# Encoder layer on one core: token tiles 4 to 7 normed column-major in PSUM, fourth block sum in PSUM banks, decay rates and token passes laid elsewhere

## The chip, the core and the metric

One core of a Trainium2 chip. The kernel is written against five engines that run side by side, each with its own queue in program order: TensorE (PE in the profile, its weight loads PEld), VectorE (DVE), ScalarE (ACT), GpSimd (POOL) and SyncE (SP, which here only issues DMAs). The metric is the device time of one execution in microseconds, median of several runs.

## The reference, cut to what matters

1024 tokens (a grid of 16 rows by 64 columns) of 1024 channels, float32. First an embedding LayerNorm, then one layer:

```
h    = layer_norm(x, emb_ln_g, emb_ln_b)
proj = h @ w_in                # 1024 x 5120: q | k | v | z_attn | u | z_lru | g_attn | g_lru
y_a  = neighbourhood_attention(q, k, v, rpb) * silu(z_attn)       # 8 heads x 64
u    = centred_depthwise_conv(u)
a    = exp(-8 * softplus(-lam) * sigmoid(gate_r(u)))              # decay of the recurrence
y_b  = (rg_lru forward + rg_lru backward)(u) * silu(z_lru)
m    = sigmoid(g_attn + b0) * (y_a @ w_ba) + sigmoid(g_lru + b1) * (y_b @ w_bb)
out  = layer_norm(alpha * h + m @ w_out, ln_g, ln_b)
```

Two things are wanted of h: column-major (channels on the partitions) as the operand of the projection, and row-major in DRAM, for `alpha * h` at the very end. The factor `8 * softplus(-lam)` (the decay rates) depends on the weights alone.

## The kernel before

**Tiles and stages.** The tokens form eight tiles of 128. Each float32 operand of a product is kept as a high part (rounded to fp32r) and a low part (the rest); a product is three matmuls, high x high, low x high, high x low (`mm3`, L127 is the subtraction that makes a low part, L133 the matmul). The projection of 34 of the column groups runs as 17 *pairs*; a pair is one 2 x 2 block product done with seven block products in place of eight. These need sums of blocks of h (T1 to T4, made once) and of the weights (s1 to s4, made for each pair).

**First stage, to about 83 us.** Tile by tile: statistics on DVE (`ln_stats`, `ln_rstd`), then the normalization. Tiles 0, 1 and 3 do it on DVE (`ln_v`); tiles 2 and 4 to 7 scale on ACT (`ln_scale`, L254) and take gain and shift on POOL (`ln_g`, four 512-wide operations, L260). `keep` stores the row-major tile to `h_d`. `turn` has TensorE transpose the tile in eight 128 x 128 steps into two PSUM banks (tile name tp, L271), ACT writes the high parts (`turn_hi`) and DVE the low parts (`turn_lo`) to the block operands B11, B12, B21, B22. For tiles 4 to 7 `t_full` makes T1, T2 and T3 and `t_last` makes T4, on DVE; `t_hi` splits on ACT and `t_lo` on POOL. In between stand the products for v (`v_part`, L327) and for half of q (`q_part`), which need nothing but finished tiles, and the splitting of the first pair's weights (`s_hi`, `s_lo`).

**The pairs, from about 83 us.** A loop over *slots*: slot 7p + k is block product k of pair p, in the order a11, a12, s2, s1, s3, s4, a22. In each slot the code issues, in this order: the copy or sum that empties the PSUM bank of the slot before (`evacuate`), the high part of a weight block of the next pair (`s_hi`), what `at(slot, 0, ...)` has put there, the product, the low part of the block of the slot before (`s_lo`), the stores that fell due two slots after their sum, a weight sum of the next pair (`s_sum`, L385) or, at k = 4, the weight loads of the pair after it, and what `at(slot, 1, ...)` has put there. Six PSUM banks serve the pairs, and two the gates of the recurrence. Product a22 adds into the bank of which `evacuate` has just read in the slot before.

**Order.** All queues are written out by hand: `manual_schedule` for PE and for DVE, ACT, POOL and SP; an instruction waits for its data at the head of its queue, with all behind it. The lists `CONV_AT`, `GATE_AT`, `LATE_AT` and `range(8, 14)` for the decay rates say in which slots the side work is issued: the convolution (`conv_stage`, from slot 14), the gates and the scans (`gate_stage`, from slot 21), the decay rates (`decay_rates`, L650 to L670, 31 operations on 8 or 16 columns on DVE and one Exp on ACT, in six portions). The first `take` (`take_q`) splits q of the other heads: sum on DVE, high part on ACT one slot later, low part on DVE and store two slots later.

**After the pairs** come attention, the merge and the output projection, which the change doesn't touch; there `z_load` reads `h_d` back.

Of the kernel before, what the change touches and what calls it, by code (L numbers as in the profile page):

```python
# [15 lines left out]
P = 128  # L16
# [27 lines left out]

BIAS_W = 7 * P

SM_CW, SM_CB, SM_GB, SM_LAM, SM_BM, SM_N = 0, 16, 20, 36, 44, 60
# [17 lines left out]


@with_exitstack
def encoder_kernel(ctx, tc, x, gb1, gb, w_qk, w_v, w_s, w_ba, w_bb, w_gate, smalls, bias, w_out, out):
    nc = tc.nc
    V, A, G, PE, SP = nc.vector, nc.scalar, nc.gpsimd, nc.tensor, nc.sync  # L70

# [39 lines left out]
    V.memset(eps_t, EPS)  # L111
    V.memset(eps_z, EPS * TWICE * TWICE)
    A.activation(warm, eps_t, AF.Sqrt)
    sm = cst.tile([P, SM_N], F32, name="sm")
# [11 lines left out]
    def lo_of(eng, lo, full, hi):  # L126
        eng.tensor_tensor(lo, full, hi.bitcast(F32), ALU.subtract)  # L127
# [48 lines left out]
    def qk_prep(m):  # L176
        qk_hi(m)
        qk_lo(m)
# [52 lines left out]
    def ln_sums(i):  # L231
        ln_stats(i)
        ln_root(i)
# [15 lines left out]
    def ln_scale(i):  # L249

        z, (st, mv, sd, ve) = xs[i], sts[i]
        ln_rstd(i)
        V.tensor_scalar(ve[:, 2:3], mv[:, 0:1], -1.0, sd, ALU.mult, ALU.mult)
        A.activation(z[:], z[:], AF.Identity, bias=ve[:, 2:3], scale=sd)  # L254

    def ln_g(i):
        z = xs[i]
        for c in range(2):
            for w, op in enumerate((ALU.mult, ALU.add)):
                G.tensor_tensor(z[:, halves[c]], z[:, halves[c]], gb_t[w][c][:], op)  # L260

    def keep(i):
        SP.dma_start(h_d[i], xs[i][:])

    tps = {}

    def turn(i, kk):
# [22 lines left out]
    def f(t, i):  # L290
        return t[:, :, ti(i)].bitcast(F32)

    def t_full(i):

        tag = ("a22", "a21", "a12", "a22")[i - 4]
        tt[i, 3] = wsp.tile([P, 4, P], F32, tag=tag, bufs=2 if tag == "a22" else 1, name=f"t3_{i}")[:]
# [3 lines left out]
        A.copy(t3, tp4(i, 0))  # L300
        V.tensor_tensor(t1, tp4(i, 0), f(B11[0], i), ALU.subtract)
        V.tensor_tensor(t1, t1, f(B11[1], i), ALU.subtract)
        V.tensor_tensor(t2, tp4(i, 1), t1, ALU.subtract)
        V.tensor_tensor(t3, tp4(i, 1), t3, ALU.subtract)

    def t_last(i):
        t4 = tt[i, 4] = tt[i, 2]
        V.tensor_tensor(t4, f(B21[0], i), t4, ALU.subtract)
        V.tensor_tensor(t4, t4, f(B21[1], i), ALU.add)

    def t_hi(i, *cs):
        for c in cs:
            A.copy(Ts[c][0][:, :, ti(i)], tt[i, c])  # L313

    def t_lo(i, *cs):
        for c in cs:
            lo_of(G, Ts[c][1][:, :, ti(i)], tt[i, c], Ts[c][0][:, :, ti(i)])

    vos, vn = {}, {}

    def v_part(i, kind, ks):

        if i not in vos:
            vos[i], vn[i] = bank(f"v{i}"), 0
        for k in ks:
            a = blocks[k // 4][i // 4][kind == "a"][:, k % 4, ti(i)]
            PE.matmul(vos[i][:], a, wv[kind == "w"][k][:], start=vn[i] == 0, stop=vn[i] == 23)  # L327
            vn[i] += 1
# [39 lines left out]
    def s_load(p, *names):  # L368
        for z, o in enumerate(names if p < N_PAIR else ()):
            if p:  # L370
                t = wsp.tile([P, 4, P], F32, tag=o, bufs=2 if o == "a22" else 1, name=f"{o}_{p}f")[:]
            else:
                if z == 0:
                    place = dict(pool=ln, tag="x", bufs=5) if o == "a21" else dict(pool=wpl, tag="ws", bufs=1)
                    both = place.pop("pool").tile([P, 2, 4, P], F32, name=f"{o}_{p}f", **place)
# [11 lines left out]
    def s_hi(p, o):  # L387
        if p < N_PAIR:
            s_w[p, o] = pair(wsp, [P, 4, P], f"w{o}_{p}", tag="w" + o)
            (G.tensor_copy if p and o in HI_POOL else A.copy)(s_w[p, o][0][:], s_a[p, o])  # L390

    def s_lo(p, o):
        if p < N_PAIR:
            hi, lo = s_w[p, o]
            lo_of(G if p and o in LO_POOL else V, lo[:], s_a[p, o], hi[:])


    K0, K1, KS, BOTH = range(4), range(4, 8), range(8), range(2)
# [10 lines left out]
    load_x(3)  # L409
    load_x(4)  # L410
    SP.dma_start(sm[:], smalls)

    warm_up(WARM[0])
    PE.transpose(clock[:, 256:272], gb_row[:], ident[:16, :16])
# [82 lines left out]
    for c, pl in zip((4, 3, 1, 2), hts):  # L497
        Ts[c] = pair(pl, [P, 4, HALF], f"ht{c}", tag=f"ht{c}")
    T1, T2, T3, T4 = (Ts[c] for c in (1, 2, 3, 4))

    def turned_in(i, kk):
        banks[0] = pst
        turn(i, kk)
        turn_hi(i, kk)
        banks[0] = ps0

    def tile_in(i):
        for kk in BOTH:
            turned_in(i, kk)

    def tile_lo(i):
        for kk in BOTH:
            turn_lo(i, kk)

    def ln_next(i):
        ln_sums(i)
        ln_scale(i)
        ln_g(i)

    keep(2)  # L520
    keep(3)
    turned_in(2, 0)
# [3 lines left out]
    v_store(0)  # L526
    turned_in(2, 1)
    turned_in(3, 1)
    ln_scale(4)
    ln_g(4)  # L530
    qk_prep(1)
    tile_lo(2)
    tile_lo(3)
    v_lo(1)
    v_store(1)
    load_x(7)
    ln_next(5)
    for kind in "hwa":
        v_part(2, kind, KS)
    keep(4)  # L540
    ln_next(6)
    v_hi(2)
    for kind in "hw":
        v_part(3, kind, KS)
    v_lo(2)
    v_store(2)
    keep(5)
    tile_in(4)
    tile_lo(4)
    ln_next(7)  # L550
    v_part(3, "a", KS)
    t_full(4)
    v_hi(3)
    v_lo(3)
    v_store(3)
    keep(6)
    q_part(0, 0, slice(256, HALF))
    tile_in(5)
    q_hi(0, 0)
    t_hi(4, 2, 1, 3)  # L560
    t_lo(4, 2, 1, 3)
    tile_lo(5)
    q_lo(0, 0)
    q_store(0, 0)
    keep(7)
    t_full(5)
    q_part(1, 0)
    q_hi(1, 0)
    q_lo(1, 0)
    q_store(1, 0)  # L570
    t_hi(5, 2, 1, 3)
    t_lo(5, 2, 1, 3)
    for kind in "hwa":
        v_part(4, kind, KS)
    tile_in(6)
    v_hi(4)
    tile_lo(6)
    v_lo(4)
    v_store(4)
    t_full(6)  # L580
    t_hi(6, 2, 1, 3)
    t_lo(6, 2, 1, 3)
    for kind in "hwa":
        v_part(5, kind, KS)
    s_load(0, "a11", "a12")
    tile_in(7)
    v_hi(5)
    tile_lo(7)
    v_lo(5)
    v_store(5)  # L590
    t_full(7)
    t_hi(7, 2, 1, 3)
    t_lo(7, 2, 1, 3)
    s_load(0, "a21", "a22")
    s_load(1, "a21")
    for kind in "hwa":
        v_part(6, kind, KS)
    v_hi(6)
    v_lo(6)
    v_store(6)  # L600
    s_load(1, "a12")
    s_sum(0, "s1", "s2", "s3", "s4")
    for kind in "hwa":
        v_part(7, kind, KS)
    v_hi(7)
    v_lo(7)
    v_store(7)
    s_load(1, "a11")
    for o in OPS[:3]:
        s_hi(0, o)  # L610
        s_lo(0, o)
    q_part(0, 1)
    for o in OPS[3:5]:
        s_hi(0, o)
        s_lo(0, o)
    q_hi(0, 1)
    q_lo(0, 1)
    q_store(0, 1)
    s_load(1, "a22")
    q_part(1, 1)  # L620
    for o in OPS[5:]:
        s_hi(0, o)
        s_lo(0, o)
    t_last(4)
    q_hi(1, 1)
    t_hi(4, 4)
    t_last(5)
    q_lo(1, 1)
    q_store(1, 1)
    for i in (5, 6, 7):  # L630
        if i > 5:
            t_last(i)
        t_hi(i, 4)
    for i in (7, 4, 5, 6):
        t_lo(i, 4)
# [5 lines left out]

    ev = pool("ev", "right")
    lru = pool("lru", "right")
    sp = lru.tile([P, 8], F32, name="sp")
    nsp = lru.tile([P, 8], F32, name="nsp")
    t0, t1, t2 = (lru.tile([P, 8], F32, name=f"sp{c}") for c in range(3))
    lam = sm[:, SM_LAM:SM_LAM + 8]

    def decay_rates():
# [144 lines left out]
    def gate_stage(t, d, slot):  # L794
# [36 lines left out]
            A.activation(g["w"][:], g["w"][:], AF.Sqrt)  # L831

        def tables():
            A.activation(warm[:], eps_t[:], AF.Sigmoid)

        def inputs():
            first = S - 1 if d else 0
# [109 lines left out]
    def gates_b(j):  # L947
# [2 lines left out]
    takes = [take_q, lambda: take_u(0), lambda: take_zg(zb_d, 0, "zb"), lambda: take_zg(za_d, 0, "za"), gates_a(0), gates_a(1),  # L950
             lambda: take_u(2), gates_b(0), lambda: take_zg(zb_d, 2, "zb"), gates_a(2), gates_b(1),
             lambda: take_k(0), gates_a(3), lambda: take_k(2), lambda: take_zg(za_d, 2, "za"), gates_b(2), gates_b(3)]
    rates = decay_rates()
# [809 lines left out]
```

## Time and profile before

| | us |
|---|---|
| median of 3 runs | 662.94 (662.82 to 663.04) |
| the profiled execution | 663.5 |
| its span in the trace | 661.7 |
| TensorE busy in it | 649.5 |
| DVE, ACT, POOL busy in it | 521.6, 389.0, 396.7 |

The span runs from the first to the last instruction that the profiler saw; 1.8 us of the execution's time lie around it. A row of a timeline has start, duration, engine, line, operation, output <- inputs, shapes and count, and in brackets the idle time of the engine before it with what ended it. A row of a group has the count, then busy time in us and mean ns of one, then idle time before. A row of the chain has start, duration and what ran.

### The profile page before, as it was taken

Reading aid. Unit: us, or ns where it says so; the run is one execution under the profiler, and the core shown is the slowest. Engines: PE = TensorE matmul, PEld = TensorE weight load, DVE = VectorE, ACT = ScalarE, POOL = GpSimd, SP = SyncE. Lnnn points to the kernel's source line nnn. Section 1 sums busy time; section 2 is a strip of 40 time slices with the busy share of each in tenths; the row PEclk is TensorE's granted clock in tenths of the full one; section 3 lists DMA queues with packets and bytes.
Section 4 is the critical chain, followed back from the end, with each engine's and each line's share of the span. In section 5 each row is a group of like instructions: output and inputs, shape, how many; then the busy total and the mean of one; then the engine's idle time right before and its main releaser. Section 6 shows DMA issues by size and latency. Waiting matters only on the chain.

```text
span 661.7 us, 9464 instructions
## 1 busy us (share of the span) xinstructions
PE 649.5 (98%) x3119; PEld 543.5 (82%) x3119; DVE 521.6 (79%) x860; ACT 389.0 (59%) x686; POOL 396.7 (60%) x311
## 2 busy tenths in 40 slices
PE   8999999999999999999999999999999999999994
PEld 7888888888888887888788888888898888888883
DVE  7978867786899599879987696277877876994776
ACT  5564433356786677777666834277777744573242
POOL 6799263434676476658556455013552549989857
PEclk9999999999999999999999999999999999999998
DMA  8747607033334133532361548898977298333023
GB/s 324 271 140 250 195 33 257 15 111 128 125 113 135 57 112 99 188 111 81 132 220 59 192 163 281 306 342 272 362 264 240 68 306 294 113 113 127 24 104 128
DMA packets 52482, 113.42 MB, mean 171 GB/s; under 512 B 5505, under 2 KB 9937, under 8 KB 50897
## 3 DMA queue, kind: packets, MB, share of 16 engines
q1 hardware_dynamic: 51968, 112.28, 49.0%
q8 instruction: 25, 0.41, 0.2%
q10 hardware_dynamic: 464, 0.53, 0.2%
q14 instruction: 25, 0.20, 0.1%
HBM read 77.11 MB, written 35.68 MB: 170 GB/s over the span
## 4 chain that ended last, share of the span: by engine, by line
PE 86%; DVE 7%; POOL 2%; issue 1%; ACT 1%; DMA 1%; POOLq 0%; DVEq 0%; ACTq 0%
PE a L133 32%; PE s L133 12%; PE mb L133 12%; PE x L133 6%; PE w L133 5%; PE v L327 4%; PE s L1107 3%; PE acc L1155 3%; PE pt L1129 3%; PE q L133 2%; PE g L805 2%; POOL x L260 1%; DVE ws_l L127 1%; DVE uc L763 1%; PE tp L271 1%
## 5 line engine op out<-in xcount | busy, mean ns | idle before, releaser
L133 PE MATMUL a<-ht_h,ws_h 128*128 128x512 f32 x136 | 53.1, 391 | 0.0
L133 PE MATMUL a<-ht_l,ws_h 128*128 128x512 f32 x136 | 52.9, 389 | 0.0
L133 PE MATMUL a<-ht_h,ws_l 128*128 128x512 f32 x136 | 52.9, 389 | 0.0
L133 PE MATMUL a<-b_l,wa_h 128*128 128x512 f32 x136 | 52.9, 389 | 0.0
L133 PE MATMUL a<-b_h,wa_h 128*128 128x512 f32 x136 | 52.9, 389 | 0.0
L133 PE MATMUL a<-b_h,wa_l 128*128 128x512 f32 x136 | 52.9, 389 | 0.0
L1117 DVE CUSTOM_DVE_ANT_0 sc<-s,bias 128x384 f32<-128x384 f32 (+1 forms) x64 | 33.5, 523 | 20.3 <-PE s L1107 11.4
L1136 ACT CAST pt_h<-pt 128x384 fp32r<-128x384 f32 x64 | 29.0, 453 | 23.8 <-PE pt L1129 19.3
L1122 ACT ACTIVATE p<-sc,summ 128x384 f32<-128x384 f32 (+1 forms) x64 | 37.9, 592 | 5.4 <-DVE summ L1117 5.0
L133 PE MATMUL mb<-ya,wb_h 128*128 128x512 f32 x128 | 39.7, 390 | 0.1
L913 POOL CAST wb_h<-wb 128x512 fp32r<-128x512 f32 x9 | 7.0, 781 | 47.2 <-DMA wb<-in_w_bb_dram 47.2
L127 DVE TENSOR_TENSOR pt_l<-pt,pt_h 128x384 fp32r<-128x384 f32 x64 | 33.3, 520 | 1.9 <-ACT pt_h L1136 1.6
L127 POOL TENSOR_TENSOR ht_l<-t,ht_h 128x512 fp32r<-128x512 f32 x16 | 21.9, 1406 | 18.2 <-ACT ht_h L313 18.2
L1521 POOL TENSOR_TENSOR z<-z,gb 128x512 f32<-128x512 f32 (+2 forms) x23 | 27.7, 1218 | 8.5 <-ACT z L1516 7.5
L327 PE MATMUL v<-wv,b_h 128*128 128x512 f32 x128 | 32.4, 395 | 0.4 <-ACT b_h L426 0.4
L1107 PE MATMUL s<-ks,qs 128*128 128x384 f32 (+1 forms) x128 | 31.7, 329 | 0.0
L133 PEld LDWEIGHTS a<-ht_h,ws_h 128*128 128x128 f32 x136 | 25.5, 188 | 5.9 <-issue 0.5
L1129 PEld LDWEIGHTS pt<-ident,p 128*128 128x128 f32 x176 | 23.1, 140 | 8.3
L133 PEld LDWEIGHTS a<-ht_l,ws_h 128*128 128x128 f32 x136 | 25.5, 188 | 5.3
L133 PEld LDWEIGHTS a<-b_h,wa_l 128*128 128x128 f32 x136 | 25.5, 188 | 5.3
L133 PEld LDWEIGHTS a<-b_h,wa_h 128*128 128x128 f32 x136 | 25.5, 188 | 5.3
L133 PEld LDWEIGHTS a<-b_l,wa_h 128*128 128x128 f32 x136 | 25.5, 188 | 5.3
(542 smaller groups left out, 2258.9 us busy)
## 6 DMA issues: line engine op xcount, KB each, us to landing
ks<-k_d SPq DMA_DIRECT2D x8, 1024.0 KB, 7.6
h_d<-x SPq DMA_DIRECT2D x8, 512.0 KB, 2.9
v_d<-vs SPq DMA_DIRECT2D x8, 512.0 KB, 3.2
q_d<-q SPq DMA_DIRECT2D x8, 512.0 KB, 3.2
ga_d<-ga SPq DMA_DIRECT2D x16, 256.0 KB, 2.1
gb_d<-gb SPq DMA_DIRECT2D x16, 256.0 KB, 2.4
k_d<-k SPq DMA_DIRECT2D x8, 512.0 KB, 5.1
qs<-q_d SPq DMA_DIRECT2D x8, 512.0 KB, 5.2
```

The lines of the kernel that those rows point to most:

```text
L127: eng.tensor_tensor(lo, full, hi.bitcast(F32), ALU.subtract)
L133: PE.matmul(o, a, b, start=first and i == 0, stop=last and i == len(prods) - 1, skip_group_check=not (first and last))
L327: PE.matmul(vos[i][:], a, wv[kind == "w"][k][:], start=vn[i] == 0, stop=vn[i] == 23)
L805: PE.matmul(o[:, n, :], w[:, 2 * d + b, :], us[b][:, n * HALF:(n + 1) * HALF], start=z == 0, stop=z == 1)
L913: G.tensor_copy(hi[:], st[:])
L1107: PE.matmul(o[:, :P * len(near(t))], q[:, t * P:(t + 1) * P], k[:, z, keys], start=z == 0, stop=z == 1)
L1117: V.tensor_tensor_reduce(s[:, :w], o[:, :w], heads[h][2][:, b0:b0 + w], -1.0, 3.0e38, ALU.add, ALU.min, accum_out=sums[h][0][:, t:t + 1])
L1122: A.activation(probs[h % 2][t][:], scs.pop((h, t))[:, :w], AF.Exp, bias=sums[h][0][:, t:t + 1], scale=-1.0, accum_out=sums[h][1][:, t:t + 1])
L1129: PE.transpose(tp[:, n * P:(n + 1) * P], probs[h % 2][t][:, z * P:(z + 1) * P], ident[:])
L1136: A.copy(pt[0][:, span(b)], tps[h, b][:, :P * len(near(b))])
L1155: PE.matmul(acc[n][:, lo - n * HALF:hi - n * HALF], vvs[h // 2][:, b, h % 2, :], pt[:, a:a + hi - lo], start=b in (1, 6) and z == 0, stop= ...
L1521: G.tensor_tensor(z, z, gbs[c, n][:, part], (ALU.mult, ALU.add)[c])
```

## The change

1. **Tiles 4 to 7 column-major.** x of these tiles is also given to the kernel transposed (`xt`; `load_xt`). The statistics still come from row-major tiles. `spread` has TensorE turn the column of means and that of reciprocal deviations into two 128 x 128 blocks of one PSUM bank (two transposes); `spread_copy` copies the second to SBUF; `centred` subtracts the mean on DVE (from PSUM) and multiplies on POOL; `affine` applies gain and shift on ACT, now a scale and a bias for each partition, eight 128-column activations into PSUM. From there `turn_hi` and `turn_lo` go on as before. 32 transposes of tiles go, as do `ln_scale` and `ln_g` for these tiles.
2. **Row-major h of tiles 4 to 7, later.** In the slots of `TOKENS_AT` x is loaded once more (`tokens_in`), scaled on ACT with the kept statistics (`tokens_scaled`), given gain and shift on POOL in four 512-wide operations, one a slot, slots 4 to 19 in all (`tokens_gained`), and stored (`tokens_out`). The gain and shift rows are loaded in slot 1 (`gains_in`).
3. **The fourth block sum** (T4) is formed in four PSUM banks and not in SBUF; its low parts move from POOL to DVE, the high part of tile 7 from ACT to DVE. The highs of T1 to T3 of tiles 4 and 5 move from ACT to POOL.
4. **Decay rates** in slots 4 to 9 and not 8 to 13; their tiles lie in the constants' pool.
5. **Weights of the first pairs:** lows of a22 and s4 of pair 0 on POOL, highs of a12 and s2 of pair 1 on ACT.
6. The order of the first stage is written anew around this: all of v for tiles 4 to 7 stands behind q of the first half.

```diff
+TOKENS_AT = ((1, 3, (4, 5, 6, 7)), (2, 6, (8, 9, 10, 11)), (9, 11, (12, 13, 14, 15)), (9, 12, (16, 17, 18, 19)))
+RATES_AT = (4, 5, 6, 7, 8, 9)
+FIRST_POOL = ("a22", "s4")
+FIRST_ACT = ((1, "a12"), (1, "s2"))
...
+    def spread(i):
+        bcp[i] = pst.tile([P, HALF], F32, tag="bank", name=f"bcp{i}")
+        for z, col in enumerate((sts[i][1][:, 0:1], sts[i][2])):
+            PE.transpose(bcp[i][:, z * P:(z + 1) * P], col.to_broadcast([P, P]), ident[:])
+    def spread_copy(i):
+        bcs[i] = wsp.tile([P, 1, P], F32, tag=f"s{i - 3}", name=f"bc{i}")
+        A.copy(bcs[i][:, 0], bcp[i][:, P:2 * P])
+    def centred(i):
+        for kk in range(2):
+            t = xts[i][:, 4 * kk:4 * kk + 4, :]
+            V.tensor_tensor(t, t, bcp[i][:, :P].unsqueeze(1).to_broadcast([P, 4, P]), ALU.subtract)
+            G.tensor_tensor(t, t, bcs[i][:].to_broadcast([P, 4, P]), ALU.mult)
+    def affine(i, *kks):
+        for kk in kks or BOTH:
+            tps[i, kk] = pst.tile([P, HALF], F32, tag="bank", name=f"tp{i}_{kk}")
+            for k4 in range(4):
+                k = 4 * kk + k4
+                g, b = (sm[:, SM_LN + 8 * z + k:SM_LN + 8 * z + k + 1] for z in range(2))
+                A.activation(tps[i, kk][:, k4 * P:(k4 + 1) * P], xts[i][:, k, :], AF.Identity, bias=b, scale=g)
+            turn_hi(i, kk)
...
-    def t_last(i):
-        t4 = tt[i, 4] = tt[i, 2]
-        V.tensor_tensor(t4, f(B21[0], i), t4, ALU.subtract)
-        V.tensor_tensor(t4, t4, f(B21[1], i), ALU.add)
+    def t_last(i, *steps):
+        for step in steps or BOTH:
+            V.tensor_tensor(tt[i, 4], (f(B21[0], i), tt[i, 4])[step], (tt[i, 2], f(B21[1], i))[step],
+                            (ALU.subtract, ALU.add)[step])
     def t_hi(i, *cs):
         for c in cs:
-            A.copy(Ts[c][0][:, :, ti(i)], tt[i, c])
+            (V.tensor_copy if (i, c) == (7, 4) else G.tensor_copy if i < 6 and c < 4 else A.copy)(Ts[c][0][:, :, ti(i)], tt[i, c])
     def t_lo(i, *cs):
         for c in cs:
-            lo_of(G, Ts[c][1][:, :, ti(i)], tt[i, c], Ts[c][0][:, :, ti(i)])
+            lo_of(G if c < 4 else V, Ts[c][1][:, :, ti(i)], tt[i, c], Ts[c][0][:, :, ti(i)])
...
+    for i in (7, 6, 5, 4):
+        tt[i, 4] = pst.tile([P, HALF], F32, name=f"t4_{i}")[:].rearrange("p (k t) -> p k t", k=4)
...
+    def tokens_scaled(i):
+        n = 2 * i - 8
+        A.activation(hw[i][:], hw[i][:], AF.Identity, bias=kept[:, n:n + 1], scale=kept[:, n + 1:n + 2])
+    def tokens_gained(i, z, c):
+        t = hw[i][:, halves[c]]
+        G.tensor_tensor(t, t, ln_row[z][:, halves[c]], (ALU.mult, ALU.add)[z])
...
+    for i, tag, (s0, s1, later) in zip(range(4, NT), ("a", "uc", "uc", "a"), TOKENS_AT):
+        at(s0, 1, lambda i=i, tag=tag: tokens_in(i, tag))
+        at(s1, 1, lambda i=i: tokens_scaled(i))
+        for slot, (c, z) in zip(later, itertools.product(BOTH, BOTH)):
+            at(slot, 1, lambda i=i, z=z, c=c: tokens_gained(i, z, c))
+        at(later[-1] + 1, 1, lambda i=i: tokens_out(i))
     rates = decay_rates()
-    for slot in range(8, 14):
+    for slot in RATES_AT:
         at(slot, 1, lambda: next(rates))
```

More of the change, by code (lines that the diff above doesn't have):

```diff
@@ L113, in encoder_kernel @@
     A.activation(warm, eps_t, AF.Sqrt)
+    kept = cst.tile([P, 8], F32, name="kept")
+    sp, nsp, t0, t1, t2 = (cst.tile([P, 8], F32, name=f"sp{c}") for c in range(5))
     sm = cst.tile([P, SM_N], F32, name="sm")
@@ L372, in s_load @@
             else:
-                if z == 0:
-                    place = dict(pool=ln, tag="x", bufs=5) if o == "a21" else dict(pool=wpl, tag="ws", bufs=1)
-                    both = place.pop("pool").tile([P, 2, 4, P], F32, name=f"{o}_{p}f", **place)
+                if z == 0 and o == "a11":
+                    both = wpl.tile([P, 2, 4, P], F32, tag="ws", bufs=1, name="a11_0f")[:]
+                elif z == 0:
+                    both = both_xt[0][:, 1].rearrange("p (z k) f -> p z k f", z=2)
                 t = both[:, z]
@@ L536, in encoder_kernel @@
     load_x(7)
[L537 to L541, printed above, removed]
-    v_hi(2)
-    for kind in "hw":
-        v_part(3, kind, KS)
+    load_xt(6)
+    load_xt(7)
+    v_part(2, "h", KS)
+    v_part(2, "w", KS)
+    spread(4)
+    spread_copy(4)
+    centred(4)
+    qk_prep(1)
+    stats_t(5)
+    v_part(2, "a", KS)
+    v_part(3, "h", KS)
+    v_part(3, "w", K0)
+    spread(5)
+    spread_copy(5)
+    stats_t(6)
+    centred(5)
+    v_hi(2)
+    v_part(3, "w", K1)
+    v_part(3, "a", K0)
+    spread(6)
+    spread_copy(6)
+    affine(4, 0)
+    ln_sums(7)
+    centred(6)
     v_lo(2)
     v_store(2)
[L547 to L552, printed above, removed]
+    affine(4, 1)
+    sts_rest(7)
+    v_part(3, "a", K1)
     v_hi(3)
+    lows_t(4)
     v_lo(3)
     v_store(3)
-    keep(6)
     q_part(0, 0, slice(256, HALF))
-    tile_in(5)
-    q_hi(0, 0)
+    t_full(4)
+    t_places(1, 2, 3)
     t_hi(4, 2, 1, 3)
     t_lo(4, 2, 1, 3)
-    tile_lo(5)
+    affine(5)
+    q_part(1, 0)
+    spread(7)
+    q_hi(0, 0)
     q_lo(0, 0)
     q_store(0, 0)
-    keep(7)
+    spread_copy(7)
+    centred(7)
+    lows_t(5)
     t_full(5)
-    q_part(1, 0)
+    t_hi(5, 2, 1, 3)
+    t_lo(5, 2, 1, 3)
+    affine(6)
     q_hi(1, 0)
@@ L570, in encoder_kernel @@
     q_store(1, 0)
[L571 to L575, printed above, removed]
+    affine(7)
+    lows_t(6)
+    t_full(6)
+    s_load(0, "a11", "a12")
+    for i in (4, 5):
+        for kind in "hwa":
+            v_part(i, kind, KS)
     v_hi(4)
-    tile_lo(6)
+    v_hi(5)
+    t_hi(6, 2, 1, 3)
+    t_lo(6, 2, 1, 3)
+    s_load(0, "a21", "a22")
     v_lo(4)
     v_store(4)
[L580 to L588, printed above, removed]
+    s_load(1, "a21")
     v_lo(5)
     v_store(5)
+    lows_t(7)
     t_full(7)
[L592 to L595, printed above, removed]
     for kind in "hwa":
@@ L600, in encoder_kernel @@
     v_store(6)
+    t_hi(7, 2, 1, 3)
+    t_lo(7, 2, 1, 3)
     s_load(1, "a12")
@@ L612, in encoder_kernel @@
     q_part(0, 1)
-    for o in OPS[3:5]:
+    for o in ("s1", "s3", "a22", "s4"):
         s_hi(0, o)
         s_lo(0, o)
+    t_places(4)
+    T1, T2, T3, T4 = (Ts[c] for c in (1, 2, 3, 4))
+    pst.release()
+    pst = tc.alloc_tile_pool(name="pst4", bufs=1, space=bass.MemoryType.PSUM, reuse_waits="tile")
+    for i in (7, 6, 5, 4):
+        tt[i, 4] = pst.tile([P, HALF], F32, name=f"t4_{i}")[:].rearrange("p (k t) -> p k t", k=4)
     q_hi(0, 1)
@@ L1733 @@
         "x": np.stack([xg[rows, cols].reshape(P, D) for rows, cols in TILES]),
+        "xt": np.stack([xg[rows, cols].reshape(P, NK, P).transpose(2, 1, 0) for rows, cols in TILES[4:]]),
         "gb1": np.stack([g["emb_ln_g"], g["emb_ln_b"]])[None],
```

104 lines of the change are left out of this document (64 added, 40 removed).

## The prediction

> **What bounds the kernel now.** I read the page first (busy shares, chain), then TensorE's waits, then the stretches.
>
> ```profile
> span 661.7 us, 9464 instructions
> ...
> PE 649.5 (98%) x3119; PEld 543.5 (82%) x3119; DVE 521.6 (79%) x860; ACT 389.0 (59%) x686; POOL 396.7 (60%) x311
> ...
> PE 86%; DVE 7%; POOL 2%; issue 1%; ACT 1%; DMA 1%; POOLq 0%; DVEq 0%; ACTq 0%
> ```
>
> ```profile
> PE tp L271 <- POOL x L260: 0.4, 1, 0.4
> PE a L133 <- DVE w L838: 0.4, 1, 0.4
> ```
>
> TensorE works 649.5 of 661.7 us and, after the first 10 us, waits twice for 0.4 us. So a TensorE instruction taken out is worth its own time, and any wait put in costs its full length. The other engines have room, though it isn't the same everywhere:
>
> ```profile
> 40.00:60.00 20.00, 19.63 (x102) 16.53 (x101) 16.54 (x29) 10.62 (x20) 19.61 (x15) 1.00 0.59 212
> 60.00:80.00 20.00, 20.00 (x94) 16.66 (x93) 15.28 (x22) 10.39 (x20) 9.47 (x8) 1.00 0.52 170
> 80.00:100.00 20.00, 20.00 (x88) 16.16 (x88) 14.55 (x21) 6.13 (x11) 11.42 (x10) 1.00 0.20 70
> 100.00:120.00 20.00, 20.00 (x90) 16.52 (x89) 15.64 (x48) 5.39 (x9) 5.91 (x8) 1.00 0.64 221
> ```
>
> Columns: stretch, length, busy time of PE, PEld, DVE, ACT, POOL, clock, DMA share, GB/s. POOL is full at 40 to 60 us (the gain and shift of tiles 4 to 7) and nearly free at 100 to 120, where the change puts that work.
>
> **The change, part by part.** *TensorE, removed.* 32 transposes (eight for each of tiles 4 to 7); added: 8 that spread a tile's mean and rstd.
>
> ```profile
> 4.21 3.41 PE gps L212 x16
> ...
> 53.95 0.87 PE tp L271 x8
> 54.82 5.47 PE v L327 x24
> 60.30 0.88 PE tp L271 x8
> ...
> 91.15 2.72 PE s L133 x12
> ...
> 99.31 11.18 PE a L133 x48
> ```
>
> In the chain eight transposes take 0.88 us, so 0.11 each: 4 x 0.88 = 3.5 us go. The added ones are of the kind of gps (a column broadcast), 0.21 each there, at a time when everything on TensorE ran at half its later rate; between 8 x 0.11 = 0.9 and 8 x 0.21 = 1.7 I take 0.9, since they stand amid full-rate work. Net -2.6.
>
> *TensorE's waits ahead of the pairs.* This one goes with POOL's passes (-0.37):
>
> ```profile
> 42.38 0.66 PE L271 MATMUL tp<-ident,x 128*128 128x128 f32 x4 [0.37 <-POOL x L260]
> ```
>
> A new one takes its place. spread(6) needs tile 6's statistics, and they stand on DVE behind those of tile 5:
>
> ```profile
> 24.90 1.28 DVE L223 BATCH_NORM_STATS2 ln4t<-x 128x6 f32<-128x512 f32 x2
> 28.01 2.47 DVE L127 TENSOR_TENSOR b_l<-tp,b_h 128x512 fp32r<-128x512 f32 x4
> 31.00 1.27 DVE L223 BATCH_NORM_STATS2 ln5t<-x 128x6 f32<-128x512 f32 x2
> 33.38 0.21 DVE L239 TENSOR_SCALAR ln5e<-ln5e 128x1 f32<-128x1 f32 x1
> ```
>
> A 512-wide DVE step is 2.47/4 = 0.6, a tile's statistics to rstd 33.59 - 31.00 = 2.6. DVE from 24.9: statistics 4 1.6, v 0.6, small ones 1.0, four lows 2.4, v 0.6, centring tile 4 1.2, tile 5 2.6, copies 0.2, tile 6 2.6: 37.7. TensorE from 25.0: 16 transposes 1.7, 44 of the products at 5.47/24 = 0.23 10.0, two spreads 0.45: 37.2. So about +0.45 (0 to 1). Behind that wait stand v of tile 3 and all that follows; the last spread waits for DVE's reading of tile 4's bank (t_full), which by the same count ends just ahead. Net of both: +0.1.
>
> *ACT* loses four 1024-wide scalings and six high copies (to POOL), and gains 32 of 128 columns.
>
> ```profile
> 26.59 0.30 ACT L229 ACTIVATE ln4e<-ln4m,few 128x1 f32<-128x1 f32 x1
> 28.13 1.24 ACT L254 ACTIVATE x<-x,ln4e 128x1024 f32<-128x1024 f32 x1 [0.27 <-DVE ln4e L253]
> ...
> L280 ACT CAST b_h<-tp 128x512 fp32r<-128x512 f32 x15 | 8.2, 590 | 5.4 <-PE tp L271 5.4
> ```
>
> No row has 128 columns: between 0.30 (one column) and 0.59 (512); on the line between the two rows of scalings, 0.30 + 127/1023 x 0.94 = 0.42, which I take. 13.4 us added, 8 removed, over 50 us in which ACT is half idle: nothing, and if that cover were gone, up to 5 us. ACT begins tile 4 behind the third spread, near 38; a tile is 8 x 0.42 and three copies at 0.5, so 4.9, and six other copies stand between: tile 7 ends near 38 + 19.6 + 3 = 61. v of tile 7 is due at 37.7 and 0.23 of spread, 4 + 24 products of tile 3 and q at 0.23 with 24 of 256 columns at half that (9.3), another spread and three tiles at 5.5: 63.8. So it is in time by 2 to 3 us.
>
> *DVE* gains eight centrings, four lows of the fourth sum (from POOL) and a high copy, 13 x 0.6 = 7.8, and gives two weight lows to POOL (1.2): +6.6 over the 60 us in which it waited some 13. The fourth sums stand behind the last q, and their PSUM banks are asked for only in slot 3 of the pairs, 8 us on: 0 (up to +1).
>
> *The pairs.* From here a slot is one product of 2.72 us. Four `a` products from 99.31 took 11.18 where 4 x 2.72 is 10.88: a22 of pair 0 waits for a late DVE, itself late by POOL's lows of the fourth sum. With these gone, -0.25 (0 to -0.3). Now the moved work: POOL has a 512-wide token operation in each of slots 4 to 19, and the decay rates' 31 small DVE operations come in slots 4 to 9. Each is hidden if one looks at busy shares only. The rows around speak against it (columns: start, duration, engine, line):
>
> ```profile
> 94.14 1.29 POOL L127 TENSOR_TENSOR wa_l<-a_1f,wa_h 128x512 fp32r<-128x512 f32 x1
> 95.37 3.12 POOL L390 CAST ws_h<-s_1f 128x512 fp32r<-128x512 f32 x3
> ...
> 110.61 0.61 POOL L390 CAST ws_h<-s_2f 128x512 fp32r<-128x512 f32 x1 [0.85 <-POOL wa_l L127]
> 113.34 0.62 POOL L390 CAST ws_h<-s_2f 128x512 fp32r<-128x512 f32 x1 [2.11 <-PE s L133]
> ```
>
> ```profile
> 94.21 1.76 DVE L127 TENSOR_TENSOR wa_l<-a_1f,wa_h 128x512 fp32r<-128x512 f32 x1 [4.22 <-POOL wa_h L390]
> 95.90 1.10 DVE L385 TENSOR_TENSOR s_1f<-a_1f,s_1f 128x512 f32<-128x512 f32 x1
> 96.92 1.09 DVE L127 TENSOR_TENSOR ws_l<-s_1f,ws_h 128x512 fp32r<-128x512 f32 x1
> ...
> 110.66 0.58 DVE L657 TENSOR_TENSOR sp<-sp,sp 128x8 f32<-128x8 f32 x1
> 113.17 0.17 DVE L662 TENSOR_TENSOR sp<-sp,sp 128x8 f32<-128x8 f32 x1
> 113.37 0.61 DVE L663 TENSOR_SCALAR sp<-sp 128x8 f32<-128x8 f32 x1
> ```
>
> A DVE operation on SBUF alone that comes while POOL works ends just behind POOL's: 94.21 + 1.76 = 95.97 behind 95.43, and two 8-column operations of 0.17 become 0.58 and 0.61, ending at 111.24 and 113.98 behind 111.22 and 113.96. POOL's casts in turn take 1.04 for 0.62. The two take turns. [...]
>
> [...] The two rows of small ones are nearest, and both were blocked to the end: I take 5.5. Two places pass it on to TensorE: s1 of pair 1 (slot 10) takes a PSUM bank of pair 0, and a22 of pair 1 (slot 13) needs DVE's sum of slot 12; queued behind them on TensorE is all the rest.
>
> Slots 14 to 20 hold the first convolution as well, three taps of 1.3 us on SBUF alone, with POOL's last six token operations: +0.8 (0 to 2.7), since DVE had these 3 us of waiting there:
>
> ```profile
> 123.69 1.28 DVE L763 SCALAR_TENSOR_TENSOR uc<-up,sm,uc 128x1024 f32<-128x1024 f32 x1 [1.03 <-ACT uc L759]
> 126.91 0.70 DVE L696 TENSOR_TENSOR a<-u,a 128x512 f32<-128x512 f32 x1 [1.94 <-PE a L133]
> ```
>
> A TensorE that stood still for over 5 us may start again at half rate, as gps did: 0 to 3.4 (half of the 7 us from its start to the end of gps); I take 1. [...]
>
> *SP's queue.* Six more loads and no fewer stores: x of tile 4 column-major ahead of the first h store, which had waited for the DMA queue anyway; in slot 9 the load of tile 7's rows waits until tile 4's store has landed (one buffer), and behind it stand the weights of pair 3 in slot 11.
>
> ```profile
> h_d<-x SPq DMA_DIRECT2D x8, 512.0 KB, 2.9
> ```
>
> 2.9 us is little more than a slot, and weights are asked for five slots ahead: 0; without that lead, 3 us once.
>
> *Sum.* -2.6 + 0.1 - 0.25 + 5.5 + 0.8 + 1.0 = +4.6. The profiled execution took 663.5 (661.7 span and 1.8 around it), 0.6 above the median of the runs; against the median, 662.9 + 4.6 = **667.5 us**.
>
> **The rivals.**
>
> [...] DVE's small operations slip between POOL's, or DVE runs far enough ahead: for it, both engines' busy shares at 80 to 120 us (78% and 30 to 57%); against it, the two blocked rows. -2.6 + 0.1 - 0.25 = -2.75: 660.2 us.
>
> *They cancel* (no change). POOL's operations hold DVE only in part and TensorE waits 2 to 4 us in all, with no half rate: about 662.9. [...]
>
> *The column-major tiles come late* (slower). It is ACT's 128-column operations at 0.6, the price of 512 columns: 32 x 0.6 = 19 us, 5.8 more than counted, and tile 7 ends near 67 where v of tile 7 is due at 63.5. It decides from 0.5 us each; at 0.6 some 3.3 us of waiting less 2.75: 663.5. With the statistics late as well (the upper 1 us), 664.3, which is slower by 0.2%.
>
> *The saving isn't one*: TensorE ahead only waits longer for DVE at the 0.4 us of L838. For it, that chain runs over DVE; against it, it begins behind a TensorE product, so it moves along. 662.5.
>
> **How the numbers follow.** A measurement of this kernel tells about 0.2%, 1.3 us, from no change. Forecast 0.55 (own range 664 to 672), port without effect 0.28, cancelled 0.10, late tiles 0.04, no saving 0.03. Faster: 0.28 and a part of the cancelled, 0.30. Slower: 0.55, nearly all of it, and half of the late tiles, 0.57. Same: 0.13. Two signs hold most, so the range goes from the bottom of the fast case to the forecast's upper bounds less the least likely tenth: 659.6 to 671.5.
>
> **What would show it.** Right: TensorE 2 to 3 us earlier at the first `a` product on split weights (80 us instead of 82.8); one wait of 0.3 to 0.8 at the spreads; then one wait of several us for DVE between 105 and 125 us, with small DVE operations of 0.5 to 1.3 us from 94 on, each ending behind a POOL operation, and matmul steps above 0.23 after it. Wrong: DVE's small operations at 0.17 to 0.2 beside busy POOL rows, and no TensorE wait there; then the time is near 660. A wait for ACT in front of v of tiles 4 to 7 would mean the late tiles.

## The result and the profile after

The changed kernel took 672.53 us (median of 6 runs, 670.96 to 674.87) where the kernel before took 662.89 on the same chip: a ratio of 1.0149, with a 95% interval of 1.0129 to 1.0169. It is 9.6 us slower (8.6 to 11.2); the forecast was 4.6 slower, and its range ended at 671.5. Runs of the changed kernel spread over 4 us, those of the kernel before over 0.3. The profiled execution, at 673.9, is 1.4 above its median; its span is 10.4 us longer than before's, and that is what the rows have to account for.

The page of the changed kernel (span; busy time, share and instructions; granted clock in tenths over 40 slices; shares of the chain that ended last):

```profile
span 672.1 us, 9492 instructions
...
PE 651.9 (97%) x3095; PEld 543.2 (81%) x3095; DVE 546.7 (81%) x875; ACT 401.6 (60%) x717; POOL 412.2 (61%) x321
...
PEclk9999999789999999999999999999999999999998
...
PE 67%; DVE 20%; issue 5%; ACT 3%; DMA 2%; POOL 1%; SPq 0%; POOLq 0%; DVEq 0%; ACTq 0%
```

VectorE is now 20% of the chain that ended last (7% before), and the clock row has a dip to 7 and 8 in the eighth and ninth of the 40 slices, 118 to 151 us. The waits of TensorE in that profile (total us, times, longest):

```profile
PE a L139 <- DVE up L757: 4.0, 1, 4.0
PE a L139 <- DVE c L766: 2.5, 1, 2.5
...
PE v L384 <- ACT b_h L485: 0.9, 1, 0.9
PE v L384 <- ACT wv L202: 0.6, 1, 0.6
PE s L1207 <- DVE m L1130: 0.5, 1, 0.5
PE bcp L294 <- DVE ln6e L245: 0.4, 1, 0.4
```

The first two are new and are single waits. TensorE's timeline shows where (start, duration, engine, line; the bracket gives the idle time ahead and what ended it):

```profile
23.11 0.28 PE L139 MATMUL q<-b_h,wqk_h 128*128 128x256 f32 x1
...
81.58 0.50 PE L139 MATMUL a<-b_h,wa_h 128*128 128x512 f32 x1 [0.26 <-DVE q L416]
...
117.28 0.39 PE L139 MATMUL s<-b_l,ws_h 128*128 128x512 f32 x1
121.64 0.80 PE L139 MATMUL a<-ht_h,wa_h 128*128 128x512 f32 x1 [3.97 <-DVE up L757]
122.23 0.63 PE L139 MATMUL a<-ht_h,wa_l 128*128 128x512 f32 x1
...
126.89 0.40 PE L139 MATMUL a<-b_h,wa_h 128*128 128x512 f32 x1
...
143.00 0.39 PE L139 MATMUL s<-b_l,ws_h 128*128 128x512 f32 x1
145.91 0.50 PE L139 MATMUL a<-ht_h,wa_h 128*128 128x512 f32 x1 [2.53 <-DVE c L766]
...
147.49 0.63 PE L139 MATMUL a<-ht_h,wa_h 128*128 128x512 f32 x1
```

Both waits are at an a22 product, the last of a pair: that of pair 1 in slot 13, for VectorE's sum of slot 12, and that of pair 2 in slot 20. A step is 0.227 us elsewhere. The first wait cost 121.64 - 117.28 - 0.23 = 4.1 us, and its twelve products took 5.25 us where 12 x 0.227 is 2.7: 2.5 more. The second cost 2.7, and the products from 147.49 on come at 0.43 us as well, another 1.6. Together 10.9 us, in 34 us of the program.

What VectorE was doing, in the same profile, and GpSimd beside it:

```profile
109.27 1.23 DVE L733 TENSOR_SCALAR sp<-sp 128x8 f32<-128x8 f32 x1
110.53 0.17 DVE L732 TENSOR_TENSOR sp<-sp,sp 128x8 f32<-128x8 f32 x1
...
113.32 1.22 DVE L733 TENSOR_SCALAR sp<-sp 128x8 f32<-128x8 f32 x1
...
115.12 1.22 DVE L733 TENSOR_SCALAR sp<-sp 128x8 f32<-128x8 f32 x1
116.26 0.68 DVE L757 TENSOR_TENSOR up<-u,a 128x512 f32<-128x512 f32 x1
```

```profile
109.18 1.29 POOL L1041 TENSOR_TENSOR hw<-hw,ln_row 128x512 f32<-128x512 f32 x1
...
113.22 1.29 POOL L1041 TENSOR_TENSOR hw<-hw,ln_row 128x512 f32<-128x512 f32 x1
...
115.03 1.29 POOL L1041 TENSOR_TENSOR hw<-hw,ln_row 128x512 f32<-128x512 f32 x1
```

The three 8-column operations of 1.2 us began just behind a token pass and ended just behind it: 109.27 + 1.23 = 110.50 behind 109.18 + 1.29 = 110.47, 114.54 behind 114.51, 116.34 behind 116.32. Free, such an operation takes 0.17. From 92 to 123 us VectorE's timeline in this profile shows no idle time: ahead of the first wait it was late because its operations took longer, not because it waited for data. Grouped (count | busy us, mean ns | idle before), first the kernel before, then the changed one:

```profile
L763 DVE SCALAR_TENSOR_TENSOR uc<-up,sm,uc 128x1024 f32<-128x1024 f32 x3 | 4.2, 1396 | 1.0 <-ACT uc L759 1.0
L663 DVE TENSOR_SCALAR sp<-sp 128x8 f32<-128x8 f32 x9 | 2.0, 220 | 0.3
L662 DVE TENSOR_TENSOR sp<-sp,sp 128x8 f32<-128x8 f32 x9 | 1.5, 165 | 0.2
```

```profile
L833 DVE SCALAR_TENSOR_TENSOR uc<-up,sm,uc 128x1024 f32<-128x1024 f32 x3 | 6.9, 2308 | 0.0
L733 DVE TENSOR_SCALAR sp<-sp 128x8 f32<-128x8 f32 x9 | 4.7, 523 | 0.3
L732 DVE TENSOR_TENSOR sp<-sp,sp 128x8 f32<-128x8 f32 x9 | 4.3, 479 | 0.2
```

The eighteen operations of the series alone grew from 3.5 to 9.0 us, the three taps of the convolution from 4.2 to 6.9, and the taps' 1.0 us of idle time ahead of them is gone.

### The profile page after: what moved, and what is told of

Its sections match the earlier page's. It is cut to its first block, busy times and chain, and to the rows that moved or that the text cites. A ratio compares the mean times of both kernels' runs of the same rounds, so it can differ in the third digit from the quotient of the medians.

```text
span 672.1 us, 9492 instructions
## 1 busy us (share of the span) xinstructions
PE 651.9 (97%) x3095; PEld 543.2 (81%) x3095; DVE 546.7 (81%) x875; ACT 401.6 (60%) x717; POOL 412.2 (61%) x321
## 4 chain that ended last, share of the span: by engine, by line
PE 67%; DVE 20%; issue 5%; ACT 3%; DMA 2%; POOL 1%; SPq 0%; POOLq 0%; DVEq 0%; ACTq 0%
PE a L139 23%; PE mb L139 12%; PE s L139 8%; PE x L139 6%; PE w L139 5%; PE acc L1255 3%; PE s L1207 3%; DVE ws_l L133 3%; PE pt L1229 3%; DVE uc L833 2%; PE v L384 2%; DVE wa_l L133 2%; PE g L875 2%; ACT tp L313 1%; DMA g<-gb_d 1%
## 5 line engine op out<-in xcount | busy, mean ns | idle before, releaser
L139 PE MATMUL a<-ht_h,wa_h 128*128 128x512 f32 x68 | 28.6, 420 | 6.8 <-DVE up L757 4.0
```

Of the source, the lines that this page charges most:

```text
L139: PE.matmul(o, a, b, start=first and i == 0, stop=last and i == len(prods) - 1, skip_group_check=not (first and last))
```

## The experiments

Theory: GpSimd's token passes and VectorE's SBUF operations hold each other up, the 8-column ones at the price of a whole pass each (1.23 us for 0.17); without the passes, both waits (4.0 + 2.5 = 6.5 us) and the slow products behind them go. What the recorded texts call the port is the author's name for this: the traces show when the operations begin and end, and no port. Rivals: another part of the change (loads, ScalarE's scaling, GpSimd's queue) makes VectorE late; the passes alone do it, without the rates; the slow products have a cause of their own. Ratios below are to the kernel before in runs on the same chip, where it took 663.9 us; 0.001 is 0.66 us.

**Without the passes, without the rates, without either.** The edits (the second also leaves out the six calls of the rates):

```diff
-        for slot, (c, z) in zip(later, itertools.product(BOTH, BOTH)):
-            at(slot, 1, lambda i=i, z=z, c=c: tokens_gained(i, z, c))
```
```diff
-    rates = decay_rates()
-    for slot in RATES_AT:
-        at(slot, 1, lambda: next(rates))
+    at(RATES_AT[0], 1, no_rates)          # sp and nsp set to constants
```

> The changed kernel without the sixteen GpSimd passes over the token tiles 4 to 7 (their gain and shift are left out; their loads, their scaling on ScalarE and their stores stay). [...] 672.5 - 6.5 - 4.3 = 661.7, between 661 and 663. Rival (other parts of the change, such as the token loads in SP's queue or ScalarE's scaling, hold VectorE up): the waits stay and the time is above 671.

> The changed kernel without the decay rates: the small operations of slots 4 to 9 and their one exponential are left out, two constant columns stand in their place (so the recurrence has other rates). Theory: the wait at pair 1 was the small operations ending behind GpSimd's passes one by one, so it falls below 0.5 us together with its slow products; the wait at pair 2 comes from the convolution's taps beside the passes of slots 14 to 19 and stays, 2 to 2.7 us plus 1 to 1.6 us of slow products: 672.5 - 6.5 = 666, between 665 and 667. Variant: the second wait is the first one's backlog carried on, then both go and it takes about 662. Rival (the 512-column operations alone suffice): the wait at pair 1 stays above 2.5 us and the time above 669.

> The changed kernel without the sixteen passes and without the decay rates: what is left of the change is the column-major norming, the block sum in PSUM, and the moved loads. Theory: the rates cost nothing without the passes, so it equals the kernel without the passes alone within 0.4 us, about 661.7; if the saving of the first stage is 2.7 us as forecast and not the 1.2 us that the one profile showed, 660.2. Rival: a cost of the rest of the change remains and it is above 663.

Measured: without the passes 0.9987 (0.9978 to 0.9997), without the rates 1.0014 (1.0005 to 1.0024), without either 0.9991 (0.9981 to 1.0000). From the last: the rates alone cost nothing, the passes alone 1.5 us, both together 10.5. So 9.0 of the 10.5 us are neither's own but their meeting, as the theory has it. Without the rates, the wait at pair 1 is gone and one remains at pair 2 (waits of TensorE):

```profile
PE a L139 <- DVE c L766: 1.4, 1, 1.4
```

It is smaller than the 2 to 2.7 us expected, and no product behind it was slow, so the kernel lies 0.9 us above before where 3.1 was expected. And "neither" is not the 660 us that the forecast's first-stage saving would make of it: the rest of the change is worth 0.6 us (0 to 1.3).

**The passes put into the kernel before.** Two loads in slot 1 give them idle buffers to work on; nothing else is changed, and their result is read by nobody.

```diff
+    def side_pass(n):
+        t = side[0][:, halves[n % 2]]
+        G.tensor_tensor(t, t, side[1][:, halves[n % 2]], (ALU.mult, ALU.add)[n // 2 % 2])
+
+    for n in range(16):
+        at(4 + n, 1, lambda n=n: side_pass(n))
```

> The kernel before with nothing changed but an added load of two idle SBUF tiles in slot 1 and sixteen GpSimd passes over one of them, one in each slot from 4 to 19, whose result nobody reads. Theory: the passes alone, beside the decay rates in slots 8 to 13 and the convolution in slots 14 to 20, put waits of TensorE for VectorE of 2 to 7 us in all into slots 10 to 21, with products at 0.43 us behind them: 662.9 + 4 to 11, so 667 to 674. Rival (GpSimd's passes cost VectorE nothing by themselves): within 0.4 us of the kernel before.

Measured: 1.0149 (1.0134 to 1.0165), as slow as the changed kernel. Its waits of TensorE:

```profile
PE a L133 <- DVE up L687: 6.3, 1, 6.3
...
PE a L133 <- DVE c L696: 1.0, 1, 1.0
PE v L327 <- ACT wv L196: 0.6, 1, 0.6
```

The same two products wait. So the passes beside the rates, which stand in slots 8 to 13 here, are enough without any other part of the change; moving the rates to slots 4 to 9 was not what hurt. The last row matters for the first stage: this kernel's first stage is that of before, and it too has the wait for `wv` that the changed kernel showed and the profile of before did not.

**GpSimd's casts on ScalarE.** VectorE's low parts read casts that stand in GpSimd's queue behind the passes; that is the rival to the theory.

```diff
-            (G.tensor_copy if p and o in HI_POOL and (p, o) not in FIRST_ACT else A.copy)(s_w[p, o][0][:], s_a[p, o])
+            (G.tensor_copy if p > 3 and o in HI_POOL else A.copy)(s_w[p, o][0][:], s_a[p, o])
```

> The changed kernel with GpSimd's casts for pairs 1 to 3 (thirteen, of 0.6 to 0.85 us) done on ScalarE, so that in slots 0 to 19 no VectorE instruction reads what GpSimd wrote. Theory (the port): the decay rates' small operations still end behind the token passes, the wait at pair 1 stays at 2.5 to 4 us and that at pair 2 at 1.5 to 2.7 us: 668 to 672.5. Rival (the queue: VectorE's low parts wait for casts that stand behind the token passes in GpSimd's queue): the waits at pairs 1 and 2 fall below 0.5 us each and the time is 662 to 664.

Measured: 1.0135 (1.0115 to 1.0155). The waits stay, 1.8 us at pair 1 and 3.7 at pair 2, 5.5 in all where the changed kernel had 6.5; the first is smaller and the second larger than expected. At pair 1 no VectorE instruction is left that reads what GpSimd wrote, and VectorE's timeline shows no idle time ahead of the first wait: there the wait doesn't need the queue. At pair 2 the run does not rule a queue out, for the cast only went from one to another. It now stands on ScalarE behind a scaling that waits 6.0 us for the token loads, and VectorE stands idle for it:

```profile
122.97 1.37 DVE L133 TENSOR_TENSOR ws_l<-s_2f,ws_h 128x512 fp32r<-128x512 f32 x1 [2.28 <-ACT ws_h L448]
```

**The waits filled.** Idle products stand where TensorE waited:

```diff
+        if (p, k) in FILLERS:             # (1, 6): 18, (2, 6): 11
+            w = psd.tile([P, 2, HALF], F32, tag="gates", name=f"fill{p}")
+            for _ in range(FILLERS[p, k]):
+                PE.matmul(w[:, 0, :], B11[0][:, 0, :P], B11[0][:, 0, :], start=True, stop=True)
```

> The changed kernel with idle products added on TensorE ahead of the last product of pair 1 (18, so 4.1 us) and of pair 2 (11, so 2.5 us), into PSUM that nobody reads: they fill the two waits. VectorE ends as late as before. Theory (the slow steps of 0.43 us come from TensorE having stood still): the steps behind both products are 0.227 us, the 2.4 and 1.6 us of slow products go and the waits are taken by the idle products: 672.5 - 4.0 = 668.5, between 668 and 669.5. Rival (the slow steps have another cause, such as late operands): the time stays at 672.5 or rises.

Measured: 1.0102 (1.0087 to 1.0117), 3.1 us less than the changed kernel instead of 4.0. TensorE's timeline:

```profile
118.09 4.24 PE L1112 MATMUL fill<-b_h 128*128 128x512 f32 x18
122.17 0.49 PE L140 MATMUL a<-ht_h,wa_h 128*128 128x512 f32 x1
122.50 0.39 PE L140 MATMUL a<-ht_h,wa_l 128*128 128x512 f32 x1
```

The product starts as late as ever (122.17 for 121.64), but behind a first step of 0.33 the steps are 0.23 us. From 119 to 127 us (busy time and count of each engine, granted clock, DMA share), first in the changed kernel, then in the filled one, the clock is 1.00 where it was 0.57:

```profile
119.00:127.00 8.00, 5.36 (x13) 4.24 (x14) 4.60 (x10) 2.48 (x2) 2.09 (x3) 0.57 0.98 321
```
```profile
119.00:127.00 8.00, 8.00 (x36) 6.49 (x35) 5.06 (x11) 3.25 (x4) 2.49 (x4) 1.00 0.95 312
```

So the slow products (0.43 us a step) came from standing still: with the wait filled, there are none. The 0.9 us that is missing is more than covered by a new wait of 2.1 us in slot 16, for a copy by ScalarE. In ScalarE's timeline of the filled kernel it stands behind the convolution's first operation, which waits for a token tile's store out of the buffer that it takes over:

```profile
130.87 1.24 ACT L830 ACTIVATE uc<-up,sm 128x1024 f32<-128x1024 f32 x1 [3.64 <-DMA h_d<-hw]
132.01 0.56 ACT L1089 COPY u<-a 128x512 f32<-128x512 f32 x1
```

**The way the second wait came about.** VectorE's lateness at slot 12 delays a query store on SP's queue (to 117.56 us), behind it the token loads of tiles 6 and 7 (118.14), and ScalarE then waits for these (10.68 us). In the changed kernel, SP's queue, then ScalarE and GpSimd:

```profile
117.56 0.52 SPq L793 DMA_DIRECT2D q_d<-q  x1
118.14 1.48 SPq L1033 DMA_DIRECT2D hw<-in_x_dram  x2
```
```profile
123.59 2.62 ACT L1037 ACTIVATE hw<-hw,kept 128x1024 f32<-128x1024 f32 x2 [10.68 <-DMA hw<-in_x_dram]
```
```profile
124.91 1.29 POOL L1041 TENSOR_TENSOR hw<-hw,ln_row 128x512 f32<-128x512 f32 x1 [6.02 <-ACT hw L1037]
...
146.31 1.73 POOL L1041 TENSOR_TENSOR hw<-hw,ln_row 128x512 f32<-128x512 f32 x1
```

The eight passes of tiles 6 and 7, meant for slots 12 to 19, so all ran from 124.9 to 148 us, beside the convolution. And GpSimd's queue held VectorE up: a weight's cast stood behind the first of these passes (126.13 to 126.75), and VectorE, which needs it for the low part, stood idle:

```profile
126.79 1.77 DVE L133 TENSOR_TENSOR ws_l<-s_2f,ws_h 128x512 fp32r<-128x512 f32 x1 [3.40 <-POOL ws_h L448]
```

So two things made VectorE late at pair 2, this idle time and the passes beside the taps. The edit gives the loads one slot of lead:

```diff
-TOKENS_AT = (..., (9, 11, (12, 13, 14, 15)), (9, 12, (16, 17, 18, 19)))    # buffers a, uc, uc, a
+TOKENS_AT = (..., (8, 11, (12, 13, 14, 15)), (8, 12, (16, 17, 18, 19)))    # buffers a, uc, r, uc
```

> The changed kernel with the token loads of tiles 6 and 7 one slot earlier (slot 8 for slot 9; tile 6 in the idle buffer of the gates' first column, so that the load waits for no store), and nothing else. In the changed kernel they were issued at 118.1 us behind a query store that waited for VectorE, ScalarE waited 10.7 us for them, and the eight passes of tiles 6 and 7 ran from 124.9 to 148, all beside the convolution; without the decay rates they were issued at 109.3 and the second wait was 1.4 us instead of 2.5. Theory (VectorE's lateness comes back through SP's queue): loads near 113, ScalarE's wait 5 us or less, passes from 119 on, the first wait unchanged at 3.5 to 4.5 us, the second 0.5 to 1.5 us: 668.5 to 671. Rival (the second wait is the port's load whatever the hour of the passes): both waits as they were and 672 to 673.

Measured: 1.0122 (1.0106 to 1.0139), by its middle 1.8 us less, though the intervals overlap. ScalarE waits 5.8 us (5 or less was expected), the passes start at 119.8, VectorE has no idle time for a cast any more, and the second wait falls from 2.5 to 1.1 us and brings no slow products; the first grew from 4.0 to 5.0, outside what was expected. The second wait does depend on the hour of the loads; how much of it was the idle time and how much the passes, no run separates. Why the first grew was not followed up.

**Versions meant to be faster.** The rates go to GpSimd behind its work of the first stage (they ran from 83 to 93 us, ahead of the first token pass), the passes of tile 7 go behind the convolution, and tiles 6 and 7 take the buffers of the edit above; then two orders are changed; then the banks; then, in place of the banks, the query block:

```diff
-            V.tensor_tensor(t2[:], t2[:], t1[:], ALU.mult)      # and the rest of the series, slots 4 to 9
+            G.tensor_tensor(t2[:], t2[:], t1[:], ALU.mult)      # called behind t_last(4)
-TOKENS_AT = (..., (9, 12, (16, 17, 18, 19)))
+TOKENS_AT = (..., (9, 16, (21, 22, 23, 24)))
```

> The changed kernel, all of its work done, with the decay rates taken off VectorE (all but six of their operations on GpSimd, and into the end of the first stage, where GpSimd stood idle for 8.75 us) and with the token passes of tile 7 moved from slots 16 to 19 to slots 21 to 24, behind the convolution. Theory: neither of the two waits for VectorE is left, so it takes what the changed kernel without the passes took, 0.1% below the kernel before: 662.0 to 662.6 where before is 662.9. If passes in slots 12 to 15 still reach the taps, a wait of 0.5 to 1.5 us stays at pair 2: 663 to 664.5. Rival (GpSimd's passes cost by something other than VectorE's small operations and taps): above 666.

Measured: 0.9991 (0.9982 to 1.0001). The 9.6 us are back, with all of the change's work done; both waits are gone.

```diff
-    v_part(3, "a", K0)                       # K1 stood behind sts_rest(7)
+    v_part(3, "a", KS)
     spread(6)
...
-    t_lo(5, 4)
     q_lo(1, 1)
     q_store(1, 1)
+    t_lo(5, 4)
```

> The kernel of the run before, and two orders changed in the first stage: the low half of the last query block is formed ahead of the last-but-two low part of the fourth block sum (the first product of the pairs waited 0.3 to 0.8 us for it), and the spread of tile 6 stands behind all of v's block 3 instead of before its last twelve products (the spread waited 0.4 us for the reciprocal root). Theory: 0.5 to 1.0 us less than the run before, 661.2 to 662. Rival (TensorE meets the same wait one product later): the same within 0.2 us.

Measured: 0.9993 (0.9984 to 1.0003), no difference, as the rival had it. A wait of 0.46 us for the query block stayed at the first product of the pairs.

```diff
-    psd = tc.alloc_tile_pool(name="psd", bufs=1, ...)
     banks[0] = tc.alloc_tile_pool(name="ps6", bufs=6, ...)
+    psd = tc.alloc_tile_pool(name="psd", bufs=1, ...)
```

> The kernel of the run with the two orders changed, and the PSUM banks of the pairs given out in another order: the first product of the pairs takes the bank that v's tile 6 left 6 us earlier, not that of the query block whose low half VectorE forms last (for which TensorE waited 0.3 to 1.0 us in every kernel with the change). Theory: the wait goes, 0.4 to 0.8 us less than the two runs before it: 0.9980 to 0.9988 of the kernel before, 661.7 to 662.2 where before is 662.9. Rival (TensorE meets VectorE's lateness again at the first operand of the pairs or at the next bank): the same as those two within 0.2 us, 0.9990 to 0.9995.

Measured: 1.0111 (1.0097 to 1.0125), 8 us worse and outside both expectations. The wait at the first product is gone, and the second product now has a bank in which a fourth block sum still stands:

```profile
PE a L139 <- DVE ht_l L133: 6.4, 1, 6.4
```

```diff
+    q_hi(0, 1); q_lo(0, 1); q_store(0, 1)    # stood behind this loop
     for o in ("s1", "s3", "a22", "s4"):
```

> The kernel with the two orders changed (banks as in the changed kernel), and the query block's two evacuations moved ahead of the splits of s1 and s3 of pair 0, so that VectorE forms its low half about 1.5 us earlier and its bank is free when the first product of the pairs begins. Theory (that product waits for the query block's low half only): the wait of 0.5 to 1.0 us at the start of the pairs goes and no other takes its place before slot 3, where s1 is read: 0.9980 to 0.9988 of the kernel before, 661.7 to 662.2 where before is 662.9. Rival (VectorE has no slack at the end of the first stage, so what is put ahead there makes the splits or the fourth block sum late by as much): 0.9990 to 0.9997, with a wait for VectorE in slots 1 to 6.

Measured: 0.9989 (0.9980 to 0.9998): 0.7 us (0.1 to 1.3) less than the kernel before, the best of those that do all the work, though its interval overlaps those of the two versions of 0.9991 and 0.9993. It lies between what the theory and the rival gave. The wait for the query block went, and one of 0.6 us for VectorE's low part of a fourth block sum came one product later, which is the rival's sign: VectorE has no slack there.

## Why the prediction was wrong

The sign, VectorE's small operations held up by GpSimd's passes as the cause of the first wait, and the two stretches (slots 4 to 13 and 14 to 20) were right; the sum was 5.8 us short of the profile's 10.4, and five terms make that up. TensorE's timeline of before, for the first stage:

```profile
22.12 0.28 PE L133 MATMUL q<-b_h,wqk_h 128*128 128x256 f32 x1
...
82.78 0.39 PE L133 MATMUL a<-b_h,wa_h 128*128 128x512 f32 x1
```

and ScalarE's of the changed kernel, tile 7's second half:

```profile
60.45 1.97 ACT L313 ACTIVATE tp<-xt,sm 128x128 f32<-128x128 f32 x4
62.45 0.59 ACT L339 CAST b_h<-tp 128x512 fp32r<-128x512 f32 x1
```

- *TensorE's restart at half rate, +1.0 (0 to 3.4): the step that failed most.* It was counted for one wait, at a part of its cost, and for a stand of over 5 us; 4.0 and 2.5 were enough. It came at both waits (0.43 us a step for 0.227), 2.5 and 1.6 us, 4.1 in all; the filled kernel shows that these are a price of standing still. +3.1.
- *The convolution beside the last passes, +0.8 (0 to 2.7).* It measured 2.7, its upper bound. The forecast took six passes there, on time; the steps *SP's queue: 0* and "2.9 us is little more than a slot" missed that a late VectorE delays a query store, that one the token loads, and these ScalarE, so that eight passes fell on the convolution and VectorE stood idle for 3.4 us. Where the passes were not held up so (without the rates, in the kernel before with the passes, and with the earlier loads) the second wait was 1.0 to 1.4 us and brought no slow products (0.23 us a step behind those of 1.4 and 1.1). +1.9.
- *VectorE held up in slots 4 to 13, +5.5.* No run shows the term of 5.5 us of waiting: the runs showed a wait of 4.1, at the second of the two places named, and the eighteen operations of the series 5.5 us longer (3.5 to 9.0). The working was that of the traces: whole passes as the price of 8-column operations (1.23 us for 0.17). Slot 10, the first place, brought no wait. -1.4.
- *The first stage, -2.6 + 0.1.* From the first q product to the first a product, before took 82.78 - 22.12 = 60.7 us and the changed kernel 81.58 - 23.11 = 58.5: 2.2 less, and the 0.3 short of the forecast is the wait for a query block at the first product of the pairs. But that q product came 1.0 later, since TensorE waited for `wv` and `b_h`; the kernel before with the passes has the wait for `wv` too. Over the profiles, the first q product begins at 22.4 to 23.2 us in the eleven kernels with the change, at 22.1 and 22.6 in the two with the first stage of before: it differs between executions, and whether the change has a share in it is not shown. +1.3 in the profiles compared.
- The rest is +0.9: 0.3 at the first T product of pair 0 and 0.7 at the first score of the attention, which waits for VectorE's first operation of the merge (`m`), itself behind a load. That last wait stood in seven of the twelve new profiles, 0.5 to 1.2 us, and not in the others; what decides it stays open.
- The other steps held. No wait for ScalarE stands ahead of v of tiles 4 to 7: four 128-column operations took 1.97 us, 0.49 each where 0.42 was estimated, and tile 7 was done at 63.0, where 61 was forecast and 63.8 due. The new wait at a spread was 0.4. The 0.25 us at pair 0's a22 is gone.

The saving of 2.2 us in the stage does not reach the end whole: without passes and rates, 0.6 us (0 to 1.3) is left of it. In that kernel's profile the first `a` product begins only 0.8 us earlier than before (82.01 for 82.78), since the first q product came 1.0 later and a wait of 0.7 for the query block stands ahead of the pairs; the T product (0.3) and `m` (0.8) then take more than the rest. That execution was 0.7 above its median, and no run took these waits away one by one.

The forecast's own range ran to 672, still 0.5 short of the result; the range given left out its upper end as unlikely. It took the terms as if each went its own way. Here they were one event: the waits of 4.0 and 2.5 us brought products at 0.43 us a step for 0.227 with them, and the lateness behind the first made the next stretch wait too.

## What to carry to other kernels

Work that hides by busy shares is costed where it meets other work: here a chain of 8-column VectorE operations beside 512-column GpSimd passes paid up to a whole pass for each meeting (1.23 us for 0.17), though the rates alone cost nothing and the passes alone 1.5 us. A wait on TensorE is costed with the slow products behind it (here 2.5 us behind 4.0 and 1.6 behind 2.5, none behind 1.4), and with what the late engine's own outputs hold up on other queues (here ScalarE for 10.7 us). Before such work is placed, look for the stretch in which one of the two engines stands idle.

## What the runs showed of the hardware beyond that

Slow products followed waits shorter than the 5 us expected. In the kernel with the casts on ScalarE, TensorE's timeline has eight products at 0.43 us behind a wait of 1.8:

```profile
119.54 0.64 PE L139 MATMUL a<-ht_h,wa_h 128*128 128x512 f32 x1 [1.80 <-DVE up L757]
119.98 0.63 PE L139 MATMUL a<-ht_h,wa_l 128*128 128x512 f32 x1
...
122.97 0.49 PE L139 MATMUL a<-ht_l,wa_h 128*128 128x512 f32 x1
123.30 0.39 PE L139 MATMUL a<-ht_h,wa_h 128*128 128x512 f32 x1
```

The waits of 1.4 us (without the rates) and 1.1 (with the earlier loads) had none, and neither had the longer one of 2.1 us in the filled kernel, behind which the steps are 0.23 us from 133.03 on: in these runs the length of a wait alone does not decide. Behind the 2.5 us of the changed kernel they began 1.6 us after the restart (147.49), while those of 1.8 and 4.0 us were followed by them at once. The slow stretches lasted 2.7 us (the casts' kernel, behind 3.7 us) to 6.1 (the kernel with the earlier loads, behind 5.0 us). What decides whether slow products come, and when, no run here shows.

The series of the rates on GpSimd, 128 x 8 each, began about every 0.3 us (84.61, 84.90, 85.24 us) where VectorE's begin every 0.20 (114.90, 115.09, 115.30 us in the kernel before). In GpSimd's idle time, 83 to 93 us, they cost TensorE nothing that was seen: no wait for GpSimd of 0.2 us or more.
